# Host-laid inputs for the first mixer: one load per unit, one tile for the small vectors

## The chip, the cores and the metric

The kernel runs on one core of a Trainium2 chip. The metric is the device time of one execution in microseconds (us): 2438.17 us before the change, the median of three runs (2437.43 to 2439.51). The engines are named as in the profile: PE is TensorE's matmul side, PEld its weight load, DVE VectorE, ACT ScalarE, POOL GpSimd, SP the engine that here only issues DMAs.

## The reference, cut to what matters

A network of two blocks on 256 tokens of width 1024. The first block has two layers, each a modulated mixer and a mixture of experts; the second block (attention and feed-forward layers) follows on its output. The change touches what the first layers' mixers read.

```python
def first_block(x, c, ada_w, ada_b, ...):
    c_act = jax.nn.silu(c)
    for i in range(DEPTH):
        mods = (c_act @ ada_w[i] + ada_b[i])[:, None, :]
        sh_m, sc_m, g_m, sh_f, sc_f, g_f = jnp.split(mods, 6, axis=-1)
        h = x * (1.0 + sc_m) + sh_m
        ...  # i = 0: conformer_conv, i = 1: short_gated_conv
        x = layer_norm(ALPHA * x + (1.0 + g_m) * y, mix_ln_g[i], mix_ln_b[i])
        h = x * (1.0 + sc_f) + sh_f
        y = hierarchical_moe(h, ...)
        x = layer_norm(ALPHA * x + (1.0 + g_f) * y, ffn_ln_g[i], ffn_ln_b[i])

def conformer_conv(h, w_in, b_in, w_dw, b_dw, ln_g, ln_b, w_out, b_out):
    a, g = jnp.split(h @ w_in + b_in, 2, axis=-1)
    u = a * jax.nn.sigmoid(g)
    u = causal_depthwise_conv(u, w_dw) + b_dw      # 31 taps
    u = jax.nn.silu(layer_norm(u, ln_g, ln_b))
    return u @ w_out + b_out
```

## The kernel before, in words

All weights stream from HBM through one class, `Stream`, in units of up to 1 MB (128 partitions by 2048 float32). SP issues their loads in one order that `first_units` and `second_units` lay down; a load is issued as soon as one of 15 tiles of SBUF (11, and 4 that are lent) is free (`pump`, `_load`, line 93). Most units are then split on the chip into a high and a low float16 half: ACT writes the high half (`_high`, line 120), DVE the low half (`_split`, line 107), and only the two together free the float32 tile. A unit is given back by `done` when its last matmul has been written into the program.

Each engine works through its own list in the order in which the Python code wrote it (the schedule is manual). An instruction that waits holds up all that stands behind it on its engine.

The DMAs signal their end on eight counters, named DMAHW0 to DMAHW7, which are given out in turn. A DMA waits, before SP issues it, for the end of the DMA eight places earlier, which had the same counter. So SP never has more than eight of its DMAs outstanding.

`first_mixer` is the first layer's mixer. It calls `first_consts`, which issues the first loads: the vector `c`, 12 rows of biases, the tokens `x` (1 MB), then fourteen units by `pump(0)` (one tile is kept free); then 21 small DMAs: the taps `a_w_dw` as 31 rows, rows of biases and norms, router weights. Then PE turns rows into columns: the biases (lines 440 and 441), the tokens (line 451, into `xT`, which is the tile `cz`). The two closures `taps` and `vectors` that it returns do the same for the taps (line 462, 160 small matmuls) and for the other vectors (line 479), later.

The head then runs four rounds `n`. `modulation(n)` multiplies two units of `ada_w` by the activated `c` (line 711), turns the result (line 719), and DVE reduces it to columns (lines 721 and 723). `modulate` scales the tokens by them (lines 558 and 560) into the halves `xh` and `xl` (lines 564 and 565), and two units of `a_w_in` are split. `rows(k)` multiplies a split unit by the tokens, 36 matmuls of line 736. In rounds 2 and 3 one of the closures is run ahead of `rows(2 * n)`:

```python
for n in range(4):
    m = modulation(n)
    next(m)
    if n:
        rows(2 * n - 1, m)
    next(m, None)
    if n > 1:
        consts.pop(0)(cb)
    rows(2 * n)
w.split(*u["i3"])
rows(7)
```

Then come the gates (line 773), the convolution on DVE (lines 776 and 779) and PE (lines 788 and 796) beside further modulations (line 522), the norm, the output projection (line 662) and the router; then the experts (lines 1182 and 1204) read 96 MB of weights per layer. The second mixer is `gated` (line 901), which reads `b_w_in` in 12 units.

Of the kernel before, what the change touches and what calls it, by code (L numbers as in the profile page):

```python
# [167 lines left out]
class Kernel:  # L168
# [220 lines left out]
    def first_consts(self, pool, early, keep, xT):  # L389
        nc, a = self.nc, self.a  # L390
        c8 = early.tile([P, 8], F32, name="c8")
        vb = pool.tile([40, D], F32, name="vb")
# [17 lines left out]
        nc.scalar.activation(ca, c8, AF.Silu)  # L410
        self.rw = []
        for l in range(2):
            t = [early.tile([P, 8, n], F32, name=f"rw{l}{n}") for n in (4, 32)]
# [4 lines left out]
            self.rw.append([t, b])
        self.lnT = pool.tile([P, 2, 2, 8], F32, name="lnT")
        for i, nm in enumerate(("mix_ln_g", "mix_ln_b")):  # L420
            nc.sync.dma_start(self.lnT[:, i], dap(a[nm], 0, [[8, P], [D, 2], [1, 8]]))
# [22 lines left out]
        for j in range(2):
            nc.vector.tensor_scalar(self.vb0[:, j], pt[:, 96 + j : 112 : 2], float(j), XS, op0=OP.add, op1=OP.mult)
        for k in range(0, 8, 2):
            px = self.acc()
# [4 lines left out]
            nc.scalar.activation(xT[:, k : k + 2].rearrange("p k t -> p (k t)"), px, AF.Copy)

        def taps(pt):


            pq = [q for q in range(8) if q not in self.VECTOR_Q]
            for r in range(4):
                for n, q in enumerate(pq):
                    for s in range(4):  # L460
                        c0 = 256 * (q // 2) + 64 * s + q % 2
                        nc.tensor.matmul(pt[32 * r : 32 * r + 32, (4 * n + s) * 8 : (4 * n + s) * 8 + 8], wd[:, c0 : c0 + 63 : 2],
                                         self.ident[:31, r:32:4], start=True, stop=True, tile_position=(0, 32 * r))
            for n, q in enumerate(self.VECTOR_Q):
                c0 = 256 * (q // 2) + q % 2
                nc.tensor.transpose(pt[:, 256 + 31 * n : 287 + 31 * n], wd[:, c0 : c0 + 255 : 2], self.ident[:31, :31])
            w4 = self.w4 = keep.tile([P, 32 * len(pq)], F32, name="w4")
            nc.vector.tensor_copy(w4, pt[:, : 32 * len(pq)])
            t = keep.tile([P, 31 * len(self.VECTOR_Q)], F32, name="taps")
            nc.vector.tensor_copy(t, pt[:, 256 : 256 + 31 * len(self.VECTOR_Q)])  # L470
            self.taps = {q: t[:, 31 * n : 31 * n + 31] for n, q in enumerate(self.VECTOR_Q)}
            m32 = self.m32 = keep.tile([P, 32], F32, name="m32")
            nc.vector.tensor_reduce(m32, self.ident.rearrange("p (r j) -> p j r", r=4), axis=AX.X, op=OP.add)

        def vectors(pt):
            self.vqT = pool.tile([P, 8, 8], F32, name="vqT")
            for q in range(8):
                h, i = divmod(q, 2)
                nc.tensor.transpose(pt[:, q * 8 : q * 8 + 8], vq[:, 256 * h + i : 256 * h + 256 : 2],
                                    self.ident[32:40, 32:40])  # L480
            nc.vector.tensor_copy(self.vqT, pt[:, :64].rearrange("p (k r) -> p k r", k=8))
# [4 lines left out]
            for l, (t, b) in enumerate(self.rw):  # L486
                r = pool.tile([P, 8, 36], F32, name=f"rw{l}")
                nc.vector.tensor_copy(r[:, :, :4], t[0])
                nc.vector.tensor_copy(r[:, :, 4:], t[1])
                self.rw[l] = (r, b)  # L490
# [1508 lines left out]
```

## Time and profile before

| what | value |
|---|---|
| median of 3 runs | 2438.17 us |
| the profiled execution | 2437.86 us |
| its span, first to last instruction | 2436.2 us |
| PE busy in the span | 2340.5 us (96%) |
| PEld, DVE, ACT, POOL busy | 57%, 49%, 37%, 6% |
| moved by DMA | 709.90 MB, mean 291 GB/s |
| mean granted TensorE clock | 0.988 of full speed |

Outside the span lie 1.7 us of the profiled execution. The share of PE is a mean over stages with different limits, and matmuls are pipelined, so a busy PE is not PE at its peak. What a stage is worth is read from that stage: which engine waits in it, and for what. All times in the rows are us from the start of the span.

### The profile page before, as it was taken

The page shows a single profiled execution, that of the slowest core. Times are in us where ns is not written, and L with a number is a line of the kernel's source. Part 1 is how long each engine was busy: PE and PEld are TensorE (multiplying, and loading weights), DVE is VectorE, ACT ScalarE, POOL GpSimd, SP SyncE. Part 2 cuts the span into 40 slices and gives each one's busy share as a digit, 9 for nine tenths or more (in the row PEclk, how much of TensorE's full clock was granted, in tenths as well). Part 3 has the DMA queues.
Part 4 walks back from the last instruction along what each step waited for, and adds up shares of the span by engine and source line. Part 5 has one row for each costly group of instructions (what it writes and reads, how often), then busy time and mean ns, then how long its engine had stood idle before and what let it go on. Part 6 is the DMA issues. An engine that isn't in the chain of part 4 may idle for free.

```text
span 2436.2 us, 37932 instructions
## 1 busy us (share of the span) xinstructions
PE 2340.5 (96%) x16219; PEld 1379.4 (57%) x16219; DVE 1195.0 (49%) x1718; ACT 897.1 (37%) x1222; POOL 138.3 (6%) x212
## 2 busy tenths in 40 slices
PE   7979999999999999999979999999999999999998
PEld 5534433344386343344358845548878875554985
DVE  2864222111266222111167577867556567877654
ACT  3342111111153111111144447664444445676442
POOL 0100000000000000000020021110000002111000
PEclk8989999999999999999999999999999999999999
DMA  8978999999998999999986454546647554445751
GB/s 277 412 314 331 425 425 425 425 425 425 416 378 312 394 424 425 425 425 425 425 308 211 163 183 150 185 149 248 207 156 259 189 181 164 150 160 178 247 167 69
DMA packets 191032, 709.90 MB, mean 291 GB/s; under 512 B 15054, under 2 KB 50382, under 8 KB 134026
## 3 DMA queue, kind: packets, MB, share of 16 engines
q1 hardware_dynamic: 187850, 698.50, 74.4%
q10 hardware_dynamic: 3008, 8.92, 1.0%
q8 instruction: 129, 2.11, 0.4%
q14 instruction: 45, 0.37, 0.0%
HBM read 706.33 MB, written 1.05 MB: 290 GB/s over the span
## 4 chain that ended last, share of the span: by engine, by line
PE 56%; issue 23%; DMA 8%; DVE 3%; ACT 1%; POOL 0%; ACTq 0%; POOLq 0%; DVEq 0%; SPq 0%
PE ps L1454 19%; PE ps L1576 9%; PE ps L1182 5%; PE acc L1434 5%; PE acc L1415 4%; DMA w<-in_e_w_up 3%; DMA w<-in_e_w_gate 3%; PE ps L901 3%; PE ps L1204 2%; DMA w<-in_e_w_down 2%; DVE w L107 1%; PE acc L1676 1%; PE ps L662 1%; PE ps L1136 1%; PE acc L1824 1%
## 5 line engine op out<-in xcount | busy, mean ns | idle before, releaser
L107 DVE SCALAR_TENSOR_TENSOR w<-w,w 128x2048 f16<-128x2048 f32 (+3 forms) x239 | 525.4, 2212 | 235.4 <-ACT w L120 235.1
L120 ACT ACTIVATE w<-w 128x2048 f16<-128x2048 f32 (+3 forms) x239 | 434.7, 1832 | 249.4 <-PE ps L1454 140.0
L1454 PEld LDWEIGHTS <-w 128*128 128x128 f16 x4992 | 460.9, 112 | 12.0 <-DVE w L107 2.4
L1454 PE MATMUL ps<-xh,w 128*128 128x256 f16 (+1 forms) x3328 | 378.4, 257 | 1.7 <-DVE w L107 1.6
L1236 DVE SCALAR_TENSOR_TENSOR hid<-ps,ws,sil 128x512 f32<-128x512 f32 x32 | 24.1, 752 | 471.3 <-PE ps L1182 471.3
L1182 PE MATMUL ps<-w,xl 128*64 128x512 f32 x1024 | 239.2, 598 | 12.1 <-DMA w<-in_e_w_gate 12.1
L1182 PE MATMUL ps<-w,xh 128*64 128x512 f32 x1024 | 237.1, 595 | 13.4 <-DMA w<-in_e_w_gate 11.2
L1204 PE MATMUL ps<-w,hT 128*64 128x512 f32 x1024 | 234.1, 596 | 6.7 <-DMA w<-in_e_w_down 3.5
L1454 PE MATMUL ps<-xl,w 128*128 128x256 f16 (+1 forms) x1664 | 222.8, 257 | 1.9 <-DVE xl L317 1.9
L1576 PE MATMUL ps<-w,xh 128*128 128x512 f16 (+2 forms) x896 | 195.3, 362 | 0.5 <-ACT xh L316 0.5
L1182 PEld LDWEIGHTS ps<-w,xl 128*64 128x64 f32 x1024 | 78.7, 137 | 155.0 <-issue 123.4
L1182 PEld LDWEIGHTS ps<-w,xh 128*64 128x64 f32 x1024 | 78.0, 137 | 156.3 <-issue 127.6
L1204 PEld LDWEIGHTS ps<-w,hT 128*64 128x64 f32 x1024 | 80.5, 137 | 136.1 <-issue 112.5
L1211 ACT ACTIVATE yh<-y 128x512 f16<-128x512 f32 x64 | 40.3, 630 | 256.0 <-DVE y L1210 256.0
L1576 PEld LDWEIGHTS <-xh 128*128 128x128 f16 x896 | 85.4, 98 | 85.6 <-issue 2.4
L1210 DVE TENSOR_TENSOR y<-ps,g 128x512 f32<-128x512 f32 x64 | 44.0, 688 | 166.7 <-PE ps L1204 166.7
L1192 ACT ACTIVATE hT<-ps 128x512 f32<-128x512 f32 x32 | 19.1, 597 | 270.1 <-PE ps L1190 270.1
L289 POOL TENSOR_SCALAR rv<-bnmv 128x1 f32<-128x1 f32 x20 | 16.7, 835 | 1749.5 <-DVE bnmv L302 1749.5
L1434 PE MATMUL acc<-w,hh 128*128 128x512 f16 x384 | 114.2, 379 | 0.0
L1576 PE MATMUL ps<-w,xl 128*128 128x512 f16 (+2 forms) x448 | 106.1, 362 | 0.0
L1415 PE MATMUL acc<-w,hh 128*128 128x512 f16 x320 | 95.2, 379 | 0.0
L1434 PE MATMUL acc<-w,hl 128*128 128x512 f16 x192 | 72.8, 379 | 0.0
(387 smaller groups left out, 2874.8 us busy)
## 6 DMA issues: line engine op xcount, KB each, us to landing
w<-in_e_w_gate SPq DMA_DIRECT2D x128, 1024.0 KB
w<-in_e_w_up SPq DMA_DIRECT2D x128, 1024.0 KB
w<-in_e_w_down SPq DMA_DIRECT2D x128, 1024.0 KB
w<-in_ffn_in SPq DMA_DIRECT2D x80, 1024.0 KB
w<-in_w_in SPq DMA_DIRECT2D x50, 1024.0 KB
w<-in_ffn_out SPq DMA_DIRECT2D x44, 1024.0 KB
w<-in_ada_w SPq DMA_DIRECT2D x40, 1024.0 KB
w<-in_b_w_in SPq DMA_DIRECT2D x12, 1024.0 KB
```

What stands on the lines that cost most here:

```text
L107: self.nc.vector.scalar_tensor_tensor(h[:, 1, :n], t[:, :n], WS, h[:, 0, :n], op0=OP.mult, op1=OP.subtract)
L120: self.nc.scalar.activation(h[:, 0, :n], t[:, :n], AF.Copy, scale=WS)
L662: nc.tensor.matmul(pt, X[tx][:, 2 * h + i, c * P : c * P + P], t[:, tw, i * D + n * 512 : i * D + n * 512 + 512], start=(h == 0 and i == 0 ...
L901: nc.tensor.matmul(pt[:, o + t0 : o + t1], wk, xk, start=(t0 == 0 and o == 0 and k == 0 and m == 0), stop=(t1 == S and o == S and k == 7 a ...
L1182: nc.tensor.matmul(pt[64 * e : 64 * e + 64], XT[j][:, 4 * h + k, 64 * e : 64 * e + 64], W[e][:, k * 512 : k * 512 + 512], start=(h == 0 an ...
L1204: nc.tensor.matmul(banks[n][64 * e : 64 * e + 64], hT[j][:, 2 * h + i, 64 * e : 64 * e + 64], W[e][:, i * D + n * 512 : i * D + n * 512 + ...
L1210: nc.vector.tensor_mul(y[:, sl], banks[n], G[:, sl])
L1211: nc.scalar.activation(yh[:, sl], y[:, sl], AF.Copy, scale=XS)
L1415: nc.tensor.matmul(accs[c][n], H[tx][:, 2 * h + f, c * P : c * P + P], ho[:, tw, f * D + n * 512 : f * D + n * 512 + 512], start=(j == 0 a ...
L1434: nc.tensor.matmul(accs[c][n], H[tx][:, 2 * h + f, c * P : c * P + P], ho[:, tw, f * D + n * 512 : f * D + n * 512 + 512], start=(j == 0 a ...
L1454: nc.tensor.matmul(pt[:, f % 2 * S + t0 : f % 2 * S + t1], h[:, tw, k * n + f : (k + 1) * n : nf], X[tx][:, 4 * (q % 2) + k, t0:t1], start ...
L1576: nc.tensor.matmul(pt[:, :n], X[tx][:, nk * q + k, c * P : c * P + P], h[:, tw, k * n : k * n + n], start=(q == 0 and k == 0 and tx == tw ...
```

## The change

On the host a new function `layouts` lays out eight arrays; the kernel reads them in place of the original inputs:

- `lay_x`, the tokens by channel; `lay_c`, the vector `c` beside the first 16 bias columns;
- `lay_m`, `lay_k`, `lay_t`, `lay_b`, the units of the first layer's `ada_w`, of `a_w_in` and of `b_w_in`, each unit one contiguous block;
- `lay_f`, one row of 768 values per partition: bias columns, vectors, norms and both layers' router weights. It is loaded into one tile `fix`, and `vbT`, `vqT`, `lnT` and the router weights become views of it;
- `lay_w`, the taps as the convolution wants them.

With these, the transposes of biases, tokens, taps and vectors on PE, their copies out of PSUM, and the closures `taps` and `vectors` are gone. The order of the first DMAs is new: `c`, two units, the tokens, the other units of the first `pump(0)`, then `fix`, the taps, the row vectors, `x` as rows, and four small router biases. The instructions that scale two vectors into `ba`, once at the end of `vectors`, stand in `first_consts`.

```diff
+        def block(t, i, shape, split=True):
+            n = shape[0] * shape[1]
+            return w.add([(dap(a[t], i * P * n, [[n, P], [shape[1], shape[0]], [1, shape[1]]]), None, None)], shape, split)
...
-                src = a["ada_w"]
                 for h in range(2):
-                    m = [(dap(src, 4 * h * 6 * D + j * D + 128 * k, [[8 * 6 * D, P], [6 * D, 4], [1, 256]]), 256 * j, 256 * j + 256)
-                         for j in range(2)]
-                    u.setdefault("m", []).append(w.add(m, (4, 512), False))
-            u.setdefault("k", []).append(w.add([(dap(a["a_w_in"], 128 * k * 2 * D, [[2 * D, P], [D, 2], [1, 768]]), None, None)], (2, 768)))
+                    u.setdefault("m", []).append(block("lay_m", k + h, (4, 512), False))
+            u.setdefault("k", []).append(block("lay_k", k, (2, 768)))
...
-                    u[nm] = [w.add([(dap(a["a_w_in"], j * D + 768, [[2 * D, P], [128 * 2 * D, 8], [1, 256]]), None, None)], (8, 256))
-                             for j in range(2)]
+                    u[nm] = [block("lay_t", j, (8, 256)) for j in range(2)]
                 elif nm[0] == "i":
-                    u[nm] = [cols(a["b_w_in"], 3 * D, j * D + 256 * int(nm[1]), nm != "i0") for j in (1, 2, 0)]
+                    u[nm] = [block("lay_b", 3 * int(nm[1]) + j, (8, 256), nm != "i0") for j in (1, 2, 0)]
...
-        c8 = early.tile([P, 8], F32, name="c8")
-        vb = pool.tile([40, D], F32, name="vb")
-        vq = vb[32:]
-        wd = early.tile([31, D], F32, name="wd")
+        c8 = early.tile([P, 24], F32, name="c8")
+        vb = pool.tile([21, D], F32, name="vb")
+        fix = pool.tile([P, 768], F32, name="fix")
...
-        nc.sync.dma_start(c8, a["c"].rearrange("b (p k) -> p (b k)", p=P))
-        rows(nc.sync, vb[:12], self.ROWS_B[:1])
+        nc.sync.dma_start(c8, a["lay_c"])
+        for _ in range(2):
+            self.w._load()
+        nc.sync.dma_start(xT, a["lay_x"])
+        self.w.pump(0)
+        t = keep.tile([P, 32 * 5 + 31 * 3], F32, name="taps")
+        nc.sync.dma_start(fix, a["lay_f"])
+        nc.sync.dma_start(t, a["lay_w"])
+        rows(nc.sync, vb, self.ROWS_B)
         nc.sync.dma_start(self.x, a["x"].rearrange("b (c p) d -> p (b c) d", p=P))
-        self.w.pump(0)
-        nc.sync.dma_start(wd, dap(a["a_w_dw"], 0, [[D, 31], [1, D]]))
-        rows(nc.sync, vq, self.ROWS_Q)
-        rows(nc.sync, vb[12:21], self.ROWS_B[1:])
         ca = self.ca = pool.tile([P, 8], F32, name="ca")
-        nc.scalar.activation(ca, c8, AF.Silu)
+        nc.scalar.activation(ca, c8[:, :8], AF.Silu)
+        self.w4 = t[:, : 32 * 5]
+        self.taps = {q: t[:, 160 + 31 * n : 191 + 31 * n] for n, q in enumerate(VECTOR_Q)}
+        self.vbT = fix[:, :96].rearrange("p (k r) -> p k r", k=8)
+        self.vqT = fix[:, 96:160].rearrange("p (k r) -> p k r", k=8)
+        self.lnT = fix[:, 160:192].rearrange("p (i l k) -> p i l k", i=2, l=2)
...
+            self.rw.append((fix[:, 192 + 288 * l : 480 + 288 * l].rearrange("p (k n) -> p k n", k=8), b))
...
-        self.vbT = pool.tile([P, 8, 12], F32, name="vbT")
-        pt = self.ps()
-        for k in range(8):
-            nc.tensor.transpose(pt[:, k * 12 : k * 12 + 12], vb[:12, k :: 8], self.ident[:12, :12])
-            nc.tensor.transpose(pt[:, 96 + 2 * k : 98 + 2 * k], vb[:2, k * P : k * P + P], self.ident[:2, :2])
-        nc.vector.tensor_copy(self.vbT, pt[:, :96].rearrange("p (k r) -> p k r", k=8))
         self.vb0 = pool.tile([P, 2, 8], F32, name="vb0")
         for j in range(2):
-            nc.vector.tensor_scalar(self.vb0[:, j], pt[:, 96 + j : 112 : 2], float(j), XS, op0=OP.add, op1=OP.mult)
-        for k in range(0, 8, 2):
-            px = self.acc()
-            for e in range(2):
-                for c in range(2):
-                    o = e * S + c * P
-                    nc.tensor.transpose(px[:, o : o + P], self.x[:, c, (k + e) * P : (k + e) * P + P], self.ident)
-            nc.scalar.activation(xT[:, k : k + 2].rearrange("p k t -> p (k t)"), px, AF.Copy)
...
-        def taps(pt):
...
-        def vectors(pt):
...
-            self.ba = pool.tile([P, 8, 2], F32, name="ba")
-            nc.vector.tensor_scalar(self.ba[:, :, 0], self.vqT[:, :, 0], 1.0 / INV, None, op0=OP.mult)
-            nc.vector.tensor_scalar(self.ba[:, :, 1], self.vqT[:, :, 2], 1.0 / INV, None, op0=OP.mult)
...
+        m32 = self.m32 = keep.tile([P, 32], F32, name="m32")
+        nc.vector.tensor_reduce(m32, self.ident.rearrange("p (r j) -> p j r", r=4), axis=AX.X, op=OP.add)
+        self.ba = pool.tile([P, 8, 2], F32, name="ba")
+        for j in range(2):
+            nc.vector.tensor_scalar(self.ba[:, :, j], self.vqT[:, :, 2 * j], 1.0 / INV, None, op0=OP.mult)
...
-                consts = list(self.first_consts(pool, mp, keep, z))
+                self.first_consts(pool, mp, keep, z)
...
-                    if n > 1:
-                        consts.pop(0)(cb)
...
+def layouts(v):
+    out = {}
+    out["lay_x"] = v["x"][0].T.reshape(8, P, S).transpose(1, 0, 2)
+    b0 = v["ada_b"][0].reshape(6, 8, P)[:2].transpose(2, 0, 1).reshape(P, 16)
+    out["lay_c"] = np.concatenate([v["c"].reshape(P, 8), b0], axis=1)
+    w0 = v["ada_w"][0].reshape(P, 2, 4, 6, 4, 256)[:, :, :, :2]
+    out["lay_m"] = w0.transpose(4, 1, 0, 2, 3, 5)
+    wk = v["a_w_in"][0].reshape(8, P, 2, D)
+    out["lay_k"], out["lay_t"] = wk[..., :768], wk[..., 768:].transpose(2, 1, 0, 3)
+    out["lay_b"] = v["b_w_in"][0].reshape(P, 8, 3, 4, 256).transpose(3, 2, 0, 1, 4)
...
+    out["lay_f"] = np.concatenate([t.reshape(P, -1) for t in (vb, vq, ln, *rw)], axis=1)
```

SP's list at the program's start, before: `c`, `vb` (biases), `x`, then units `w` of `ada_w` and `a_w_in` (a bracket names the counters that an instruction waits for; the first eight DMAs find theirs unused).

```order
L402 DMA c_146<-in_c 128x8
L399 DMA vb<-in_ada_b 12x1024
L404 DMA x<-in_x 128x2x1024
L93 DMA w_152<-in_ada_w 128x4x256 x2
L93 DMA w_155<-in_ada_w 128x4x256 x2
L93 DMA w_158<-in_a_w_in 128x2x768
L93 DMA w_160<-in_a_w_in 128x2x768 [waits DMAHW0_49]
L93 DMA w_162<-in_ada_w 128x4x256 [waits DMAHW1_49]
L93 DMA w_162<-in_ada_w 128x4x256 [waits DMAHW2_49]
```

SP's list at the same place, now; the last rows are the end of the first `pump(0)`, `fix` and the taps.

```order
L399 DMA c_146<-in_lay_c 128x24
L95 DMA w_150<-in_lay_m 128x2048
L95 DMA w_152<-in_lay_m 128x2048
L402 DMA cz<-in_lay_x 128x2048
L95 DMA w_155<-in_lay_k 128x1536
L95 DMA w_157<-in_lay_k 128x1536
L95 DMA w_159<-in_lay_m 128x2048
L95 DMA w_161<-in_lay_m 128x2048
L95 DMA w_163<-in_lay_k 128x1536 [waits DMAHW0_49]
L95 DMA w_177<-in_lay_m 128x2048 [waits DMAHW7_49]
L405 DMA fix<-in_lay_f 128x768 [waits DMAHW0_49]
L406 DMA taps<-in_lay_w 128x253 [waits DMAHW1_49]
```

The units move ahead of the tokens, a unit of `ada_w` is one DMA in place of two, and `fix` is the 17th DMA, the third on DMAHW0 after `c` (1st) and a unit of `lay_k` (9th).

DVE's list at the program's start, before: copies of the turned biases, then round 0 of the head (`c`, `col` the columns, `mf` the scaled tokens, `xl` the low half).

```order
L442 COPY vbT<-ps 128x96 [waits PE_49]
L445 TENSOR_SCALAR vb_249<-ps 128x8 x2
L721 TENSOR_REDUCE c_303<-ps 128x4 [waits PE_49]
L723 SCALAR_TENSOR_TENSOR col_284<-c_303,vb_249 128x2x2 [waits DVE_49]
L558 TENSOR_SCALAR mf<-cz,col_284 128x256 [waits DVE_49,Activation_49]
L565 TENSOR_TENSOR xl<-mf,xh 128x512 [waits Activation_49]
L107 SCALAR_TENSOR_TENSOR w_311<-w_158,w_311 128x1536 [waits DMAHW7_49,Activation_49]
```

DVE's list at the same place, now; `c4` is the tile that was shown as `c` in the rows above.

```order
L440 TENSOR_SCALAR vb_209<-c_146 128x8 [waits DMAHW0_49]
L440 TENSOR_SCALAR vb_209<-c_146 128x8
L442 TENSOR_REDUCE m_212<-ident 128x32 [waits Pool_49]
L446 TENSOR_SCALAR ba<-fix 128x8 [waits DMAHW0_49]
L446 TENSOR_SCALAR ba<-fix 128x8
L675 TENSOR_REDUCE c_244<-ps 128x4 [waits PE_49]
L677 SCALAR_TENSOR_TENSOR col_225<-c_244,vb_209 128x2x2 [waits DVE_49]
L512 TENSOR_SCALAR mf<-cz,col_225 128x256 [waits DMAHW3_49,DVE_49]
L519 TENSOR_TENSOR xl<-mf,xh 128x512 [waits Activation_49]
```

The two instructions on `ba`, which read `fix` and wait for its DMA, stand ahead of round 0's reduce; before, they stood behind all four rounds.

## Rows read from the trace of the kernel before

**Rows 1.** Chain that ended last, 380 to 650 us: start, length, what.

```profile
388.37 19.62 DMA w<-in_e_w_down
...
627.51 19.64 DMA w<-in_e_w_down
```

**Rows 2.** Waits of SP, 0 to 260 us: total us, times, longest.

```profile
SPq L93 <- PE ps L662: 29.7, 4, 27.1
...
SPq L93 <- PE ps L1182: 21.2, 7, 4.9
```

**Rows 3.** Windows: us, PE PEld DVE ACT POOL busy (x), clock, DMA, GB/s.

```profile
34.50:38.00 3.50, 3.41 (x17) 2.37 (x18) 1.79 (x2) 1.48 (x1) 0.00 (x0) 0.52 1.07 359
...
66.30:74.00 7.70, 7.68 (x70) 6.77 (x70) 4.53 (x9) 3.39 (x2) 3.38 (x4) 1.00 1.02 416
...
80.00:140.00 60.00, 53.38 (x585) 29.84 (x587) 54.73 (x110) 17.57 (x37) 5.91 (x3) 0.98 1.02 415
...
175.00:190.00 15.00, 14.90 (x82) 6.70 (x81) 11.66 (x21) 4.30 (x5) 0.78 (x2) 1.00 0.12 50
...
225.00:640.00 415.00, 402.63 (x2163) 167.47 (x2160) 80.75 (x166) 68.62 (x132) 0.00 (x0) 1.00 1.01 425
...
672.00:786.00 114.00, 110.84 (x883) 86.39 (x882) 77.14 (x134) 45.73 (x55) 5.57 (x13) 0.98 0.92 352
```

**Rows 4.** Waits of PE, 80 to 215 us: total us, times, longest.

```profile
PE ps L540 <- DVE col L541: 6.6, 2, 4.1
...
PEld ps L522 <- DMA w<-in_ada_w: 0.3, 1, 0.3
```

**Rows 5.** Timeline, 0 to 20 us: start, length, engine, line, what [idle before].

```profile
1.75 0.41 SPq L404 DMA_DIRECT2D x<-in_x  x1
...
6.91 3.68 PE L451 MATMUL acc<-ident,x 128*128 128x128 f32 x16 [1.62 <-DMA x<-in_x]
...
12.44 1.06 PE L711 MATMUL ps<-w,ca 128*32 128x512 f32 x8 [0.76 <-DMA w<-in_ada_w]
...
14.90 0.17 DVE L721 TENSOR_REDUCE c<-ps 128x4 f32<-128x16 f32 x1 [9.17 <-PE ps L719]
...
16.54 1.47 ACT L120 ACTIVATE w<-w 128x1536 f16<-128x1536 f32 x1
...
19.85 5.82 PEld L736 LDWEIGHTS <-w 128*128 128x128 f16 x34 [1.66 <-DVE w L107]
```

**Rows 6.** Timeline, 30 to 75 us, PE and DVE.

```profile
30.11 0.41 DVE L558 TENSOR_SCALAR mf<-cz,col 128x256 f32<-128x256 f32 x1
...
34.59 5.28 PEld L736 LDWEIGHTS <-w 128*128 128x128 f16 x34 [1.68 <-DVE w L107]
...
44.29 0.41 DVE L558 TENSOR_SCALAR mf<-cz,col 128x256 f32<-128x256 f32 x1
...
46.76 4.93 PE L462 MATMUL ps<-ident,wd 31*32 31x8 f32 x160 [0.29 <-DMA wd<-in_a_w_dw]
...
52.12 5.28 PEld L736 LDWEIGHTS <-w 128*128 128x128 f16 x36
...
63.94 1.12 PE L479 MATMUL ps<-ident,vb 8*128 8x8 f32 x8
...
66.31 7.54 PEld L736 LDWEIGHTS <-w 128*128 128x128 f16 x70 [1.21 <-DVE w L107]
```

**Rows 7.** Timeline of SP, 38 to 191 us.

```profile
38.80 0.22 SPq L399 DMA_DIRECT2D vb<-in_a_ln_b  x1
...
43.13 0.23 SPq L399 DMA_DIRECT2D vb<-in_mix_ln_g  x1
...
53.12 4.38 SPq L93 DMA_DIRECT2D w<-in_a_w_in  x4
...
160.87 29.24 SPq L93 DMA_DIRECT2D w<-in_e_w_up  x4
```

**Rows 8.** DMA of 0 to 40 us: GB/s by us, and packets.

```profile
GB/s 0 3 104 127 377 401 366 383 387 387 383 405 418 406 421 386 382 374 345 347 353 377 399 409 399 368 345 346 363 341 358 384 401 399 399 363 348 350 350 346
```

More of the change, by code (lines that the diff above doesn't have):

```diff
@@ L31 @@
 NEG = -1.0e30
+VECTOR_Q = (0, 2, 4)
 LOW = 2.0 ** 11
@@ L331 @@
     )
-    VECTOR_Q = (0, 2, 4)
     AFTER = ("F N G H", "S S F S N G S S")
@@ L400, in rows @@
                 r += n
-        nc.sync.dma_start(c8, a["c"].rearrange("b (p k) -> p (b k)", p=P))
-        rows(nc.sync, vb[:12], self.ROWS_B[:1])
+        nc.sync.dma_start(c8, a["lay_c"])
[7 more added lines that the diff above has]
+        rows(nc.sync, vb, self.ROWS_B)
         nc.sync.dma_start(self.x, a["x"].rearrange("b (c p) d -> p (b c) d", p=P))
-        self.w.pump(0)
-        nc.sync.dma_start(wd, dap(a["a_w_dw"], 0, [[D, 31], [1, D]]))
-        rows(nc.sync, vq, self.ROWS_Q)
-        rows(nc.sync, vb[12:21], self.ROWS_B[1:])
         ca = self.ca = pool.tile([P, 8], F32, name="ca")
-        nc.scalar.activation(ca, c8, AF.Silu)
+        nc.scalar.activation(ca, c8[:, :8], AF.Silu)
[4 more added lines that the diff above has]
+        self.lnT = fix[:, 160:192].rearrange("p (i l k) -> p i l k", i=2, l=2)
         self.rw = []
         for l in range(2):
-            t = [early.tile([P, 8, n], F32, name=f"rw{l}{n}") for n in (4, 32)]
             b = pool.tile([36, 1], F32, name=f"rb{l}")
-            for i, (nm, lo, n) in enumerate((("group", 0, 4), ("expert", 4, 32))):
-                nc.sync.dma_start(t[i], dap(a[f"r_w_{nm}"], l * D * n, [[8 * n, P], [n, 8], [1, n]]))
+            for nm, lo, n in (("group", 0, 4), ("expert", 4, 32)):
                 nc.sync.dma_start(b[lo : lo + n], dap(a[f"r_b_{nm}"], l * n, [[1, n], [1, 1]]))
[L418 to L421, printed above, removed]
+            self.rw.append((fix[:, 192 + 288 * l : 480 + 288 * l].rearrange("p (k n) -> p k n", k=8), b))
         self.vb = vb
@@ L454, in taps @@
-        def taps(pt):
[L457 to L473, printed above, removed]
@@ L475, in vectors @@
-        def vectors(pt):
[L476 to L481, printed above, removed]
-            self.ba = pool.tile([P, 8, 2], F32, name="ba")
-            nc.vector.tensor_scalar(self.ba[:, :, 0], self.vqT[:, :, 0], 1.0 / INV, None, op0=OP.mult)
-            nc.vector.tensor_scalar(self.ba[:, :, 1], self.vqT[:, :, 2], 1.0 / INV, None, op0=OP.mult)
[L486 to L490, printed above, removed]
@@ L492, in first_consts @@
-        return taps, vectors
+            nc.vector.tensor_scalar(self.vb0[:, j], c8[:, 8 + 8 * j : 16 + 8 * j], float(j), XS, op0=OP.add, op1=OP.mult)
+        m32 = self.m32 = keep.tile([P, 32], F32, name="m32")
[3 more added lines that the diff above has]
+            nc.vector.tensor_scalar(self.ba[:, :, j], self.vqT[:, :, 2 * j], 1.0 / INV, None, op0=OP.mult)
@@ L773, in gate @@
                     nc.vector.scalar_tensor_tensor(t[:, 30:286], pt[:, :S], self.ba[:, q, 0:1], sg, op0=OP.add, op1=OP.mult)
-                    if q in self.VECTOR_Q:
+                    if q in VECTOR_Q:
                         k = self.taps[q]
@@ L802, in first_mixer @@
                     gate(q, out[q])
-                on = [q for q in range(8) if q not in self.VECTOR_Q]
+                on = [q for q in range(8) if q not in VECTOR_Q]
                 def diagonals(n):
@@ L1976 @@
 INS = (
-    "x", "c", "ada_w", "ada_b", "a_w_in", "a_b_in", "a_w_dw", "a_b_dw", "a_ln_g", "a_ln_b", "a_w_out", "a_b_out",
-    "b_w_in", "b_w_dw", "b_w_out", "mix_ln_g", "mix_ln_b", "ffn_ln_g", "ffn_ln_b", "r_w_group", "r_b_group",
-    "r_w_expert", "r_b_expert", "e_w_gate", "e_w_up", "e_w_down", "positions_2", "w_in_2", "sink_b_2", "w_br_a_2",
-    "w_br_b_2", "w_br_c_2", "w_out_2", "ffn1_in_2", "ffn1_out_2", "ffn2_in_2", "ffn2_out_2", "ln_g_2", "ln_b_2",
-)
+    "x", "ada_w", "ada_b", "a_w_out", "a_b_out", "b_w_out", "mix_ln_g", "mix_ln_b", "ffn_ln_g", "ffn_ln_b", "r_b_group",
@@ new lines @@
+    "r_b_expert", "e_w_gate", "e_w_up", "e_w_down", "positions_2", "w_in_2", "sink_b_2", "w_br_a_2", "w_br_b_2", "w_br_c_2",
+    "w_out_2", "ffn1_in_2", "ffn1_out_2", "ffn2_in_2", "ffn2_out_2", "ln_g_2", "ln_b_2",
+    "lay_x", "lay_c", "lay_m", "lay_k", "lay_t", "lay_b", "lay_f", "lay_w",
+)
+def layouts(v):
[8 more added lines that the diff above has]
+    out["lay_b"] = v["b_w_in"][0].reshape(P, 8, 3, 4, 256).transpose(3, 2, 0, 1, 4)
+    vb = v["ada_b"].reshape(12, P, 8).transpose(1, 2, 0)
+    rows = [v["a_b_in"].reshape(2, D)] + [v[n].reshape(-1, D) for n in ("a_b_dw", "a_ln_g", "a_ln_b", "b_w_dw")]
+    vq = np.concatenate(rows).reshape(8, 4, P, 2).transpose(2, 1, 3, 0)
+    ln = np.stack([v[n].reshape(2, P, 8) for n in ("mix_ln_g", "mix_ln_b")]).transpose(2, 0, 1, 3)
+    rw = [np.concatenate([v[f"r_w_{n}"][l].reshape(P, 8, -1) for n in ("group", "expert")], axis=2) for l in range(2)]
+    out["lay_f"] = np.concatenate([t.reshape(P, -1) for t in (vb, vq, ln, *rw)], axis=1)
+    wd = np.concatenate([v["a_w_dw"][0], np.zeros((1, D), np.float32)])
+    t = wd.reshape(8, 4, 4, 4, 32, 2).transpose(1, 4, 2, 5, 3, 0).reshape(P, 8, 32)
+    by = wd[:31].reshape(31, 4, P, 2).transpose(2, 1, 3, 0).reshape(P, 8, 31)
+    pq = [q for q in range(8) if q not in VECTOR_Q]
+    out["lay_w"] = np.concatenate([t[:, pq].reshape(P, -1), by[:, list(VECTOR_Q)].reshape(P, -1)], axis=1)
+    return {n: np.ascontiguousarray(t) for n, t in out.items()}
@@ L1989 @@
     arrays, aps = {}, {}
+    values = {n: np.ascontiguousarray(v) for n, v in inputs.items()}
+    values.update(layouts(values))
     for n in INS:
-        v = np.ascontiguousarray(inputs[n])
+        v = values[n]
         arrays[f"in_{n}"] = v
```

3 lines of the change are left out of this document (removed).

## The prediction

> **What bounds the kernel now.** I read the chain of waits first. In the first experts it is PE up to 388 us and from there DMA after DMA, 19.6 us at a time, until 647 us [rows 1]. That looks as if the stream of weights set the end, so that a better stream would be worth much. The windows and the waits of SP say what the stream itself hangs on: from 225 to 640 us it moves 425 GB/s without a gap, but from 175 to 190 us it moved 50 GB/s [rows 3], because SP waited 27.1 us for line 662 to give tiles back, and later for line 1182 [rows 2]. All tiles were full by then. So the gapless stretch begins when PE gets through the first mixer, and its length is fixed by bytes: the end of the experts moves one for one with the time at which PE leaves the first mixer.
>
> What sets that time? From 80 to 140 us DVE is busy for 54.73 of 60 us [rows 3] and PE waits for it (line 540, 6.6 us), while PE's wait for weights is 0.3 us [rows 4]. This stage is a chain of DVE, PE and ACT that starts when the head is through. In the head, too, each round is a chain: PE's line 711, then DVE's reduce, the scaling, ACT's and DVE's split, then 36 matmuls of line 736. Round 0's reduce stands at 14.90 us, its main matmuls start at 19.85 us [rows 5]; those of rounds 1, 2 and 3 start at 34.59, 52.12 and 66.31 us [rows 6]. So I follow these four starts and carry what they lose or win to the end.
>
> **The change part by part.** *The taps.* In round 2 PE does 160 small matmuls (4.93 us from 46.76 us) ahead of line 736 [rows 6]. From the scaling to the main matmuls round 1 took 34.59 - 30.11 = 4.48 us; round 2's scaling is at 44.29 us, so without taps its matmuls could start at 48.77 us in place of 52.12 us: 3.35 us are won.
>
> *The vectors.* In round 3 their transposes (1.12 us from 63.94 us) lie in a wait for DVE's split of which 1.21 us are left before 66.31 us [rows 6], and DVE's copies and `ba` stood behind that split. They are worth 0; were none of it covered, the transposes would give back 1.1 us.
>
> *The tokens.* Before, PE turned them from 6.91 us for 3.68 us, and the second unit of `ada_w` landed at 12.44 us [rows 5]. Now the units come first. Taken alone this is worth about 3 us, worked out under the rivals.
>
> *The wait that comes with it.* `ba` reads `fix`. DVE's list has these two instructions ahead of round 0's reduce, with a wait for the third DMA on counter DMAHW0, and that is `fix`, the 17th DMA in SP's list, behind all of `pump(0)`. Behind the waiting instruction on DVE stand the reduce, the columns, the scaling and every split; behind the columns wait ACT's scaling and PE's line 736. Nothing in the head goes on before `fix` has landed. PE has only the two units of line 711 and four transposes to do until then.
>
> When does `fix` land? Up to its end the queue carries 12,288 bytes of `c`, eight units of `ada_w` of 1,048,576, the tokens with as many, six units of 786,432 and `fix` with 393,216: 14.56 MB. Before, such a stretch ran at about 350 to 400 GB/s with rows of 1 and 3 KB [rows 8], while experts' units, whose rows are 8 KB like the new ones, run at 425 GB/s [rows 3]. I take 425, the nearest in shape: 34.3 us. The full rate began at 4 us, 2.25 us after the tokens were issued at 1.75 us [rows 5, 8]; the first unit is now issued one place earlier, some 0.5 us, so I start at 3.5 us. The last byte is there at 37.8 us. The tokens' 1.1 MB (with what was ahead) were moved by 6.2 us by the rates of rows 8, and PE began on them at 6.91 us: 0.7 us for the landing. So `fix` is there at 38.5 us. At 350 GB/s it would be 45.8 us; a floor is below under the rivals.
>
> The Trainium skill, in "DMA: Bandwidth & Descriptors", section "Where 436 GB/s comes from", puts the limit of HBM for one core at about 358 GB/s; by that figure an estimate for `fix` is 44.9 us and for the kernel 2465 us. The trace has 425 GB/s over 250 us from HBM, so the measurement decides here.
>
> *The sum.* `fix` at 38.5 us, 0.2 us for the two instructions on `ba` (0.17 us the first, the second overlaps), the reduce at 38.7 us; 4.95 us from the reduce to the main matmuls as before (19.85 - 14.90) gives 43.65 us. Round 0 is late by 23.8 us. The later rounds keep their lengths less the taps: 23.8 - 3.35 = 20.45 us late at round 3, 86.8 us in place of 66.3. All of the head's weights are on the chip by then; the last two units of `a_w_in` and those after them follow within about 15 us and are needed later still. The DVE stage, the norm, the projection and the router move by the same 20.4 us, the stream waits for tiles as it did, and the experts end 20.4 us later.
>
> *The second mixer's loads.* `b_w_in` comes in contiguous units. There PE is busy for 110.84 of 114 us, at 352 GB/s [rows 3]; the loads are hidden, 0. If they were not, 12.6 MB at 425 in place of 352 GB/s would give back 6.1 us; I keep part of that in the range.
>
> *The clock.* Round 1's main matmuls began at a granted clock of 0.52, the 1.2 GHz level, for 3.5 us, after PE had waited for a split; round 3's, where the vectors' transposes ran in that wait, at 1.00, the 2.4 GHz level [rows 3]. Without them round 3 may start like round 1, so 1.7 us lost. I put in half, 0.9 us. If the removed taps instead left round 2 at full clock, 1.7 us would be won.
>
> So 20.45 + 0.9 = 21.3 us on the profiled execution's 2437.86 us (span 2436.2 us and 1.7 us outside), which is 0.3 us under the median: 2459 us.
>
> **The rivals.**
>
> *`fix` does not wait for its turn.* If its packets passed the units ahead, it would land much earlier. SP issues it only when the 9th DMA has landed, which is 7.6 MB into the stream: 3.5 + 17.9 + 0.7 = 22.1 us; with 2.25 us to the full rate, 0.9 us of its own bytes and 0.7 us for the landing it is there at 26 us, 12.5 us less than above: some 9 us late, 2447 us. Against it: before, the last units of 0.52 MB ended in order, about 1.45 us apart (three steps from 38.80 to 43.13 us, at each of which SP got a counter back) [rows 7], which is their size over the rate of that stretch. The Trainium skill says in "DMA: Bandwidth & Descriptors", section "Queues, rings and completion order", that descriptors are taken in ring order on each DMA engine but that the ends of DMAs need not come in the order of issue; by that rule an early end is not excluded. By the rows I see none, and give it 0.05, together with a delay that is half taken up later.
>
> *The stream takes up the delay and the kernel gets faster.* Before, the last unit of the first fill had landed at 43.13 us, and SP, held by some 20 small DMAs, issued the next at 53.12 us [rows 7]; these 10 us of idle stream are mostly filled now. If the end of the experts at 647 us hung on bytes alone, PE's delay would vanish in the stage where it waits for DMA, and the time would be 2438 - 10 = 2428 us. It decides if a tile is free when SP reaches the load that held it until 190 us (four loads took 29.24 us from 160.87 us) [rows 7]. Against it: 27.1 us of that were a wait for PE [rows 2], and the number of tiles is as before. 0.03, with it a small chance of no change.
>
> *The head gets its early start.* Without the wait on `fix` the second unit would land at 9.2 us, the first unit of `a_w_in` at 13.5 us, and the main matmuls start 3.31 us after that split begins (19.85 - 16.54): 16.8 us, 3.05 us won, with the taps 6.4 us: 2431.5 us. DVE's list speaks against it; 0.01.
>
> *It is later still.* If the stream runs at 350 GB/s as before, `fix` lands 7 us later: 2466 us; with round 3 at half clock in full and `fix` held up by the DMAs behind it, 2468 us and more. 0.06.
>
> **How the numbers follow.** My forecast, a wait of DVE until the head's data are all there, has 0.85. Its own range is 2452 to 2467 us: below, the 6.1 us of the second mixer's loads and 1.7 us of clock won; above, the stream at 350 GB/s. The range is the same, since the other cases hold only 0.15. This kernel's measurement tells a change from none at about 0.2%, 5 us. Faster by more than that: 0.03; within it 0.01; slower 0.96.
>
> **What the profile of the changed kernel would show.** DVE idle until about 38 us, put down to the DMA of `fix`; PE idle from about 10 us until after 40 us; round 0's main matmuls near 43.6 us, round 3's near 87 us; DMA at about 425 GB/s from 4 us to 38 us, then a gap; the experts' end near 668 us. The forecast is wrong if the reduce of round 0 stands before 30 us, or if the experts' end moves by much less than round 3 does.

## The result and the profile after

The changed kernel takes 2457.28 us (median of 4 runs, 2456.5 to 2458.69); the kernel before, beside it on the same chip, 2438.84 us (2437.43 to 2440.33). The ratio is 1.0077, with a 95% interval of 1.0065 to 1.0089: 18.4 us slower. The profiled execution took 2458.69 us, its span is 2457.0 us. Code lines have moved: 446 is `ba`, 665 the modulation's matmuls (before 711), 675 the reduce (721), 690 the head's main matmuls (736), 109 and 122 the splits of DVE and ACT (107 and 120), 759 GpSimd's `diag` (807), 616 the projection (662), 1134 and 1156 the experts (1182 and 1204).

The timeline of the changed kernel from 11 to 100 us, which answers to [rows 5, 6] (start, length, engine, line, what, idle before):

```profile
11.94 1.08 PE L673 MATMUL ps<-ident,adar 128*128 128x128 f32 x4 [0.81 <-ACT adar L670]
...
22.16 0.33 SPq L405 DMA_DIRECT2D fix<-in_lay_f  x1
...
38.90 0.25 DVE L446 TENSOR_SCALAR ba<-fix 128x8 f32<-128x8 f32 x2 [35.61 <-DMA fix<-in_lay_f]
39.05 0.17 DVE L675 TENSOR_REDUCE c<-ps 128x4 f32<-128x16 f32 x1
...
42.14 0.13 PEld L690 LDWEIGHTS <-w 128*128 128x128 f16 x2 [29.52 <-ACT w L122]
...
43.94 5.82 PEld L690 LDWEIGHTS <-w 128*128 128x128 f16 x34 [1.66 <-DVE w L109]
...
58.67 5.28 PEld L690 LDWEIGHTS <-w 128*128 128x128 f16 x34 [1.68 <-DVE w L109]
...
72.86 3.61 PEld L690 LDWEIGHTS <-w 128*128 128x128 f16 x34 [1.68 <-DVE w L109]
...
83.53 5.30 POOL L759 TENSOR_TENSOR diag<-m,taps 128x1024 f32<-128x1024 f32 x2
83.57 3.49 DVE L109 SCALAR_TENSOR_TENSOR w<-w,w 128x1536 f16<-128x1536 f32 x1 [0.68 <-DMA w<-in_ada_w]
87.11 10.33 PEld L690 LDWEIGHTS <-w 128*128 128x128 f16 x70 [3.41 <-DVE w L109]
```

Read it from the idle times. DVE stood for 35.61 us with `ba` at the front, and the trace names the DMA of `fix`, issued at 22.16 us. The reduce follows 0.15 us after `ba` starts, though the numbers that it sums came from PE's transposes (line 673), which ended near 13 us. PE's 29.52 us name ACT's split, but that split stood behind the same reduce: a wait is put down to the last link, and the cause is some links further back. Rounds 0 to 3 begin 24.1, 24.1, 20.7 and 20.8 us later than before.

The rate of the first 40 us, microsecond by microsecond, against [rows 8]: full from 4 us, empty after 38 us.

```profile
GB/s 0 9 134 336 418 385 393 410 442 434 412 424 412 424 451 410 451 426 418 410 424 436 426 426 442 418 426 404 410 424 412 436 406 442 418 426 381 363 61 16
```

SP's waits up to 280 us, against [rows 2], where line 662 held it for the same 27.1 us:

```profile
SPq L95 <- PE ps L616: 29.7, 4, 27.1
SPq L95 <- PE ps L1134: 21.3, 7, 4.8
```

Windows, against [rows 3], with 20 us added for the later stages (us, busy times of PE, PEld, DVE, ACT, POOL, clock, DMA share, GB/s):

```profile
86.00:95.00 9.00, 7.88 (x47) 5.99 (x48) 2.90 (x2) 2.65 (x2) 3.01 (x5) 0.62 0.60 221
195.00:210.00 15.00, 14.80 (x81) 6.57 (x81) 11.38 (x20) 5.19 (x7) 0.78 (x2) 1.00 0.01 1
245.00:660.00 415.00, 400.99 (x2150) 165.64 (x2148) 80.68 (x166) 69.46 (x133) 0.00 (x0) 1.00 1.01 425
692.00:806.00 114.00, 110.79 (x886) 87.51 (x889) 76.84 (x131) 46.69 (x57) 5.57 (x13) 0.99 0.87 348
```

The experts are the same picture 20 us later, 425 GB/s without a gap, and the second mixer has PE as busy as before (110.79 of 114 us). The projection's matmuls begin at 191.81 us in place of 170.87 (+20.9); on the chain that ended last the second mixer's line 853 stands at 693.60 us in place of 672.23 (+21.4); the span is longer by 20.8 us. What the head lost by 87 us is, to a few microseconds, what the kernel lost. The chain in the experts again runs over DMAs of 19.6 us, though its last DMA ends at 639.00 us, 8 us earlier than in [rows 1], and PE's lines carry it from there. So the sign that the forecast named, an end near 668 us, counted from the last DMA, is not to be read off this chain; its last piece of line 1156 ends 21.4 us later than the same piece before (682.6 against 661.2 us):

```profile
598.12 19.65 DMA w<-in_e_w_gate
...
617.83 21.18 DMA w<-in_e_w_down
...
664.31 6.20 PE ps L1156 x25
```

### The profile page after: what moved, and what is told of

Its sections match the earlier page's. It is cut to its first block, busy times and chain, and to the rows that moved or that the text cites. A ratio compares the mean times of both kernels' runs of the same rounds, so it can differ in the third digit from the quotient of the medians.

```text
span 2457.0 us, 37482 instructions
## 1 busy us (share of the span) xinstructions
PE 2333.2 (95%) x16016; PEld 1369.3 (56%) x16016; DVE 1194.7 (49%) x1710; ACT 894.2 (36%) x1218; POOL 135.5 (6%) x212
## 4 chain that ended last, share of the span: by engine, by line
PE 56%; issue 22%; DMA 7%; DVE 3%; ACT 1%; POOL 0%; ACTq 0%; POOLq 0%; DVEq 0%; SPq 0%
PE ps L1406 19%; PE ps L1528 9%; PE ps L1134 6%; PE acc L1386 5%; PE acc L1367 4%; PE ps L853 3%; PE ps L1156 3%; DMA w<-in_e_w_down 2%; DMA w<-in_e_w_gate 2%; DMA w<-in_e_w_up 2%; DVE w L109 1%; PE acc L1628 1%; PE ps L616 1%; PE ps L1890 1%; PE acc L1776 1%
## 5 line engine op out<-in xcount | busy, mean ns | idle before, releaser
L291 POOL TENSOR_SCALAR rv<-bnmv 128x1 f32<-128x1 f32 x20 | 16.7, 834 | 1748.6 <-DVE bnmv L304 1748.6
## 6 DMA issues: line engine op xcount, KB each, us to landing
w<-in_e_w_gate SPq DMA_DIRECT2D x128, 1024.0 KB, 19.6
w<-in_e_w_up SPq DMA_DIRECT2D x128, 1024.0 KB, 19.6
```

## Experiments

The theory: DVE's in-order list holds the whole head until `fix` lands, and the rest of the kernel moves with it. The rivals: the new layouts or the order of loads cost the time in some other way (the contiguous units, `fix` itself, the second mixer), or the stream makes up for the delay. The first four kernels were timed beside the kernel before at 2439.26 us, the last three (taps alone, `diag` held back and `ba` late again) beside it at 2438.69 us.

**`ba` late.** The changed kernel with nothing but the two instructions moved on DVE; the loads stay as they are. `scaled()` is called behind round 3's splits.

```
-        for j in range(2):
-            nc.vector.tensor_scalar(self.ba[:, :, j], self.vqT[:, :, 2 * j], 1.0 / INV, None, op0=OP.mult)
+        def scaled():
+            for j in range(2):
+                nc.vector.tensor_scalar(self.ba[:, :, j], self.vqT[:, :, 2 * j], 1.0 / INV, None, op0=OP.mult)
+        return scaled
...
+                    if n == 3:
+                        scaled()
```

> The changed kernel, but the two instructions that scale vectors into ba stand on DVE ahead of round 3's split-off matmuls again, where they stood before the change; fix is loaded at the same place in SP's list. Theory (DVE's wait for fix holds the head): the wait of 35.6 us is gone, round 0's main matmuls start near 17 us (19.85 before, 43.94 after), round 3's near 60 us, and the kernel takes 2432 us (2429 to 2437), about 25 us less than the changed kernel and 6 less than before. Rival (the loss sits in the new order of the loads or in SP's waits for counters, and the wait on DVE only fills that time): at least 2450 us, and PE waits in the head for units.

Measured: 2430.97 us (2428.59 to 2432.15), ratio to before 0.9965, interval 0.9951 to 0.9979. Its timeline, in the head:

```profile
11.66 0.17 DVE L679 TENSOR_REDUCE c<-ps 128x4 f32<-128x16 f32 x1 [8.49 <-PE ps L677]
...
16.54 5.24 PEld L694 LDWEIGHTS <-w 128*128 128x128 f16 x34 [1.66 <-DVE w L109]
...
62.39 0.23 DVE L448 TENSOR_SCALAR ba<-fix 128x8 f32<-128x8 f32 x2
```

With the same bytes in the same order, the reduce stands at 11.66 us in place of 39.05 and waits for PE; `ba` costs 0.23 us and waits for nothing. Moving two instructions takes away 26.3 us: the wait is the cause, and the layouts are not.

**`fix` first.** The other way to the same end: the instructions stay, the load moves up behind `c`.

```
         nc.sync.dma_start(c8, a["lay_c"])
+        nc.sync.dma_start(fix, a["lay_f"])
         for _ in range(2):
...
-        nc.sync.dma_start(fix, a["lay_f"])
```

> The changed kernel, with fix loaded right behind c and ahead of the first two units; ba stays where the change put it. Theory: fix lands near 5 us, before round 0's reduce, so its 0.39 MB only push the units back by 0.9 us: 2433 us (2430 to 2438). Rival (where ba stands on DVE matters by itself): near 2457 us.

Measured: 2431.4 us (2429.23 to 2432.65), ratio 0.9966, interval 0.9953 to 0.9978. `ba` runs at 4.47 us, the reduce at 13.45, round 0's main matmuls begin at 18.34: 1.8 us later than with `ba` late (1.2 later than in its second trace, below), of which the time shows 0.4.

**`fix` seventh.** A dose between the two: `fix` behind six units and the tokens, as the ninth DMA.

```
         nc.sync.dma_start(xT, a["lay_x"])
+        for _ in range(4):
+            self.w._load()
+        nc.sync.dma_start(fix, a["lay_f"])
         self.w.pump(0)
```

> The changed kernel, with fix loaded behind six units and the tokens, 7.2 MB into the stream, in place of 14.2. Theory (lateness in the head goes to the end one for one): fix lands near 21.6 us in place of 38.9, so 17.3 us less than the changed kernel: 2440 us (2437 to 2444). Rival (part of a delay is taken up by the stage that waits for DMA): the end moves by clearly less than round 0 does, 2445 us or more; or, if small delays are hidden, 2433 us.

Measured: 2439.73 us (2436.05 to 2441.22), ratio 1.0001, interval 0.9992 to 1.0011. In its timeline DVE waits half as long:

```profile
20.69 0.24 DVE L448 TENSOR_SCALAR ba<-fix 128x8 f32<-128x8 f32 x2 [17.52 <-DMA fix<-in_lay_f]
20.85 0.17 DVE L677 TENSOR_REDUCE c<-ps 128x4 f32<-128x16 f32 x1
...
25.72 6.40 PEld L692 LDWEIGHTS <-w 128*128 128x128 f16 x34 [1.66 <-DVE w L109]
```

Three points on one line: the reduce at 11.66, 20.85 and 39.05 us, the time 2430.97, 2439.73 and 2457.28 us. Of 9.2 us of delay 8.8 arrive at the end, of the next 18.2 us 17.6. The rival that the stream takes up the delay falls: it gave 2445 us or more, or 2433 us.

**The second mixer's loads strided as before.**

```
-    u[nm] = [block("lay_b", 3 * int(nm[1]) + j, (8, 256), nm != "i0") for j in (1, 2, 0)]
+    u[nm] = [w.add([(dap(a["b_w_in"], j * D + 256 * int(nm[1]), [[24 * D, P], [3 * D, 8], [1, 256]]), None, None)],
+                   (8, 256), nm != "i0") for j in (1, 2, 0)]
```

> The changed kernel, with b_w_in read in strided rows of 1 KB as before the change. Theory (the second mixer's loads are hidden by PE): within 1.5 us of the changed kernel, 2457 us, and line 853's matmuls wait for no DMA. Rival (they are worth their transfer time): up to 6 us more, 2463 us.

Measured: 2456.81 us (2452.2 to 2458.24), ratio 1.0073, interval 1.0057 to 1.009, against 1.0077 of the changed kernel. PE is busy for 110.90 of 114 us there, at 350 GB/s, against 110.79 at 348 with the units whole, and the matmuls on these units wait for no DMA in either: these loads are hidden. The stream itself is slower with strided rows, as the windows of this run and of the changed kernel show, in this order:

```profile
680.00:695.00 15.00, 14.54 (x114) 10.51 (x113) 11.21 (x20) 5.07 (x10) 4.53 (x8) 1.00 1.05 357
...
680.00:695.00 15.00, 13.46 (x83) 5.74 (x79) 9.71 (x18) 3.85 (x8) 0.77 (x2) 1.00 1.02 426
```

**Taps alone.** The kernel before, with the laid-out taps and no other part of the change.

```
-        nc.sync.dma_start(wd, dap(a["a_w_dw"], 0, [[D, 31], [1, D]]))
+        nc.sync.dma_start(td, a["lay_w"])
...
-            for r in range(4):
...
+            self.w4 = td[:, : 32 * 5]
+            self.taps = {q: td[:, 160 + 31 * n : 191 + 31 * n] for n, q in enumerate(self.VECTOR_Q)}
```

> The kernel before with the laid-out taps alone, so without the 160 small matmuls; the order of loads and every other layout as before. Theory (the 160 matmuls stand between round 1's and round 2's work on PE, 4.93 us with a wait, of which the prediction counted 3.35): round 2's 36 main matmuls begin at about 48.8 in place of 52.12, and the time is 2435.5 us (2433.5 to 2437.5). Rival A (round 2 then waits for its split, and nothing is won): 2438 to 2439.5 us. Rival B (GpSimd's diag comes earlier and lies beside a DVE split, which takes 3.5 us in place of 1.8 and brings half clock): 2437 to 2441 us.

Measured: 2432.13 us (2429.59 to 2435.34), ratio 0.9973, interval 0.9962 to 0.9983: 6.6 us won, twice what was expected, and below the expected range. From its timeline:

```profile
34.36 3.61 PEld L723 LDWEIGHTS <-w 128*128 128x128 f16 x34 [1.68 <-DVE w L107]
...
46.89 5.28 PEld L723 LDWEIGHTS <-w 128*128 128x128 f16 x34 [1.68 <-DVE w L107]
...
58.70 1.03 PEld L466 LDWEIGHTS ps<-ident,vb 8*128 8x128 f32 x8 [0.21 <-DVE xl L552]
...
61.08 9.20 PEld L723 LDWEIGHTS <-w 128*128 128x128 f16 x70 [1.21 <-DVE w L107]
...
66.01 3.79 POOL L794 TENSOR_TENSOR diag<-m,taps 128x1024 f32<-128x1024 f32 x2
...
68.61 3.33 DVE L107 SCALAR_TENSOR_TENSOR w<-w,w 128x2048 f16<-128x2048 f32 x1 [3.30 <-ACT w L120]
```

Round 2 begins 5.23 us earlier than in [rows 6]. Of that 3.35 us are the matmuls that went; 1.67 us come from round 1, which took 3.61 us here, at full clock, and 5.28 us there; 0.23 us were there when round 1 began. Round 3 then took 9.20 us in place of 7.54 and lost the 1.66 us again. Rival B came true in part: GpSimd's `diag` lay beside the next split on DVE, at 68.61 us, which took 3.33 us in place of 2.61. So 2.85 us of lead are left, as far as 125 us. By the projection it is 6.89 us, and in that stretch too it is the clock (below).

**`diag` held back.** In every kernel that takes the taps and the vectors from the host, GpSimd's `diag` runs beside round 3's first split on DVE, and that split takes 3.49 us in place of 1.76. Here, on top of `ba` late, DVE copies the taps that `diag` reads only behind `ba`, in `scaled()`; the kernel with `ba` late was run again beside it.

```
-        self.w4 = t[:, : 32 * 5]
...
+            self.w4 = keep.tile([P, 32 * 5], F32, name="w4")
+            nc.vector.tensor_copy(self.w4, t[:, : 32 * 5])
```

> The kernel with ba behind round 3's splits, and the tap numbers that GpSimd's diag reads copied by DVE right after ba, so that diag begins only when round 3's splits are issued. Theory (diag beside the DVE split slows it from 1.76 to 3.49 us, the longer PE wait then costs round 3 the full clock, 10.0 in place of 7.3 us): the split takes 1.7 to 1.8 us, round 3's 70 main matmuls begin at about 57.4 in place of 59.1, and the first split of the mixer behind them comes 1.7 to 4.5 us earlier than in the kernel with ba late; of this some is given back up to 190 us, since diag now ends later: 2427 to 2430 us. Rival A (the split is slow for a reason of its own, such as its own source): 3.4 to 3.6 us again, 2431 us. Rival B (diag itself then ends last): the tap matmuls wait for it, and the time is 2432 to 2436 us.

> The changed kernel with ba behind round 3's splits, run a second time beside the next two on the same chip. All theories: about 2431 us again (2429 to 2433), ratio near 0.997.

Measured: 2431.24 us (2427.67 to 2431.74), ratio 0.9964, interval 0.995 to 0.9978; with `ba` late 2431.1 us (2430.69 to 2432.38), ratio 0.9972, interval 0.9961 to 0.9984. No difference in the time. The trace of `ba` late, run again, around round 3:

```profile
56.35 5.29 POOL L765 TENSOR_TENSOR diag<-m,taps 128x1024 f32<-128x1024 f32 x2
56.38 3.49 DVE L109 SCALAR_TENSOR_TENSOR w<-w,w 128x1536 f16<-128x1536 f32 x1 [0.68 <-ACT w L122]
...
59.92 10.10 PEld L694 LDWEIGHTS <-w 128*128 128x128 f16 x70 [3.41 <-DVE w L109]
```

and that of the kernel with `diag` held back:

```profile
56.75 1.76 DVE L109 SCALAR_TENSOR_TENSOR w<-w,w 128x1536 f16<-128x1536 f32 x1 [0.68 <-ACT w L122]
...
58.56 9.21 PEld L695 LDWEIGHTS <-w 128*128 128x128 f16 x70 [1.68 <-DVE w L109]
...
62.21 3.78 POOL L766 TENSOR_TENSOR diag<-m,w 128x1024 f32<-128x1024 f32 x2 [5.45 <-DVE w L449]
```

Half of the expectation held: with `diag` out of the way the split takes 1.76 us, so its 1.73 us more were `diag`'s doing, and the mixer behind round 3 starts 2.3 us earlier. The other half fell: round 3 is still at 9.21 us, not 7.3, though PE's wait is short again. And with the second mixer's loads strided it had the long wait and full clock, 7.54 us for the same 70:

```profile
85.86 7.54 PEld L691 LDWEIGHTS <-w 128*128 128x128 f16 x70 [3.40 <-DVE w L109]
```

So the length of that wait alone does not set the clock.

Where did the 2.3 us go? Into PE's stretch around 135 us: in the kernel before, eight transposes of line 540, 32 matmuls of line 788 and those of line 796 behind them. One window each, from the start of that stretch. The kernel before:

```profile
137.88:143.50 5.62, 5.62 (x40) 3.12 (x44) 2.95 (x6) 1.22 (x3) 0.00 (x0) 0.50 1.03 418
```

`ba` late, run again:

```profile
133.70:139.00 5.30, 5.26 (x56) 3.25 (x60) 2.97 (x6) 1.81 (x5) 0.00 (x0) 0.70 0.27 106
```

`diag` held back:

```profile
131.48:137.00 5.52, 5.52 (x40) 3.13 (x44) 2.94 (x6) 1.22 (x3) 0.00 (x0) 0.50 0.58 231
```

Taps alone:

```profile
134.90:140.00 5.10, 5.10 (x80) 3.31 (x84) 2.93 (x6) 3.75 (x6) 0.00 (x0) 1.00 1.03 418
```

The clock there was 0.50, 0.70, 0.50 and 1.00, and the number of matmuls done in little more than 5 us (40, 56, 40, 80) follows it; line 788's 32 alone took 4.02, 2.73, 4.02 and 2.12 us. By the projection, at 170.87 us in the kernel before, the three are 6.6, 6.5 and 6.9 us earlier than before, though they began round 3 6.4, 7.8 and 5.2 us earlier.

| kernel | `ba` starts | round 0 main | round 3 main | projection | median us |
|---|---|---|---|---|---|
| before | 69.74 | 19.85 | 66.31 | 170.87 | 2438.84 |
| changed | 38.90 | 43.94 | 87.11 | 191.81 | 2457.28 |
| `ba` late | 62.39 | 16.54 | 59.14 | 163.39 | 2430.97 |
| `ba` late, again | 63.18 | 17.19 | 59.92 | 164.27 | 2431.1 |
| `fix` first | 4.47 | 18.34 | 61.08 | 165.44 | 2431.4 |
| `fix` seventh | 20.69 | 25.72 | 71.15 | 174.75 | 2439.73 |
| second strided | 38.40 | 43.43 | 85.86 | 186.06 | 2456.81 |
| `diag` held back | 61.73 | 17.46 | 58.56 | 164.42 | 2431.24 |
| taps alone | 64.50 | 19.80 | 61.08 | 163.98 | 2432.13 |

(The starts are those of one profiled execution, the time is the median of all. Second strided was profiled in its fastest one, 2452.2 us.)

`ba` late, `fix` first, `diag` held back and taps alone all beat the kernel before, by 6.6 to 8.3 us, and cannot be told apart.

## Why the prediction was right

*The wait.* `fix` was put at 38.5 us; `ba` starts at 38.90 us. What carried it was the choice of 425 GB/s for the new units: from 5 to 35 us the row of rates lies between 385 and 451. The earlier stretch's 350 to 400 GB/s belonged to its short rows: the second mixer's units alone, read in rows of 1 KB again, bring 357 GB/s in place of 426. The step from the reduce to the main matmuls was taken as 4.95 us and took 4.89. Round 0 is 24.1 us late against 23.8 forecast.

*`fix` keeps its turn.* The rival that it lands early, at 26 us, had its test in the trace: issued at 22.16 us, it was usable 16.7 us later, when all that stood ahead of it had come.

*The taps.* Between rounds 1 and 2 the delay falls from 24.08 to 20.74 us: 3.34 us against 3.35. That the same part alone is worth 6.6 us was not seen in the forecast, and its interval (4.1 to 9.3 us) leaves 3.35 out. In the one trace of each kernel the rest is PE's clock; that it is so in the median is not shown.

*The vectors and the second mixer* were put at 0. The second is shown by its own experiment. The first was not tested alone and is only argued: with `diag` held back, PE waits 1.68 us for the split where the transposes stood before, so the split would have covered their 1.1 us.

*The early start.* Without the wait, the forecast was round 0 at 16.8 us and 2431.5 us. With `ba` late they are 16.54 us and 2430.97 us. But the time is not explained by the tokens, as that rival had it, and came out by luck: taps alone, with the old order of loads, give 2432.13 us, beside 2431.1 us of `ba` late. In these two traces the early start is worth 1.2 us at round 3 (59.92 against 61.08 us) and nothing at the projection (164.27 against 163.98 us); the intervals do not tell the 1 us in the time from none. No run has the new order of loads as its only change.

*One for one.* The dose of `fix` seventh gives 8.8 of 9.2 us. SP's wait for the projection's tiles stayed at 27.1 us and the gapless stretch has the same rate.

*The size.* The sum said 21.3 us slower, and the medians say 18.4. The traces differ by 20.8 us, but they are of the slowest of the changed kernel's executions (2458.69 us) and of one of the faster of the kernel before (2437.86 us). In each of the eight measurements of kernels without the tap matmuls, the median is 1.6 to 3.2 us lower than its start of round 0 and 3.35 us for the taps would give. So the sum lacks about 2 us, within the range, in every kernel without them. A likely place is the stretch around 135 us: line 788's 32 matmuls took 4.02 us before, and 2.12 to 2.89 us in seven of the eight traces (4.02 us with `diag` held back). That this is all of it is not shown.

*The clock* is the step that failed, though 0.9 us is little. The prediction had the vectors' transposes keep PE at 2.4 GHz in round 3. Taps alone keeps these transposes, and round 3 began at half clock (9.20 us in all); second strided has none, and it was at full clock (7.54 us). The clock is the third number from the right, for taps alone up to 65 us, then for second strided:

```profile
61.08:65.00 3.92, 3.92 (x21) 2.82 (x22) 2.39 (x7) 1.46 (x1) 0.00 (x0) 0.56 1.02 406
...
85.86:93.40 7.54, 7.54 (x69) 6.78 (x70) 3.50 (x2) 3.38 (x2) 1.90 (x5) 1.00 0.41 134
```

In the changed kernel round 2 won 1.67 us, the split beside `diag` lost 1.73 and round 3 itself 2.8; some 2.3 us came back between 150 and 192 us. At the projection 0.2 us of all this are left (20.9 us late, against 20.7 at round 2) where 0.9 was put in: that the error stayed small is luck, since gains and losses of 2 to 3 us cancelled. What decides where PE falls to 1.2 GHz is left open: the runs show only that it moves from one stretch to another when the work is shifted by a few microseconds.

*Not foreseen* was `diag` beside round 3's split, which no list shows, since it is a meeting of two engines in time. The kernel before has one too, one split later: there `diag` began at 70.73 us and the split at 72.18 us took 2.61 us in place of 2.29.

## What to carry to other kernels

When small tensors are gathered into one load, look up on every engine who reads it first and what stands behind that reader: two instructions of 0.23 us in all, put ahead of a reduce, cost 26 us because their data came 17th in the queue, and moving either the reader back or the load forward undid it. Where a change shifts work by a few microseconds in a chain with many short waits, compare medians and not the stages of single traces: here the same 34 weight loads took 3.61 or 5.28 us in rounds 1 and 2 and the same 70 took 7.54 to 10.33 us in round 3, by the clock, and the executions of one kernel were up to 6 us apart.
